# A hybrid GLA and attention step on one core: bounds of output rows and weights as sums of magnitudes on ScalarE, decays by their own exponential, another table of priorities

## The chip, the cores and the metric

The kernel runs on one core of one Trainium2 chip. The metric is the device time of one execution in microseconds (us); smaller is better. The engines of a core are named as the profile names them: PE (TensorE, matrix products; PEld are its weight loads), DVE (VectorE), ACT (ScalarE), POOL (GpSimd) and SP (SyncE, which only issues transfers here). Data is staged in SBUF; products land in PSUM banks of 128 x 512 fp32.

## The reference

One inference step through two layers, each adding its gated output to the rows `x` (256 context rows and 1024 sample rows of width 1024): bidirectional gated linear attention (GLA), then softmax attention. The part that the change touches is the GLA layer:

```python
def gla_mixer(h, w_in, wa1, wa2, ba, onorm, w_out, s0):
    proj = h @ w_in
    q, k, v, gate = jnp.split(proj, [...], axis=-1)
    def decay(d):
        z = ((h @ wa1[d]) @ wa2[d] + ba[d]).astype(jnp.float32)
        return (jax.nn.log_sigmoid(z) / GLA_TAU).reshape(B, T, GLA_HEADS, GLA_DK)
    o_f, s_f = gla_chunked(q, k, v, decay(0), s0[:, 0])
    o_b, s_b = gla_chunked(flip(q), flip(k), flip(v), flip(decay(1)), s0[:, 1])
    o = rms_norm(o_f + flip(o_b), onorm).reshape(B, T, GLA_VD).astype(h.dtype)
    y = (o * jax.nn.silu(gate)) @ w_out
```

Inside `gla_chunked` each chunk needs `exp(b)` and `exp(-b)` of the running sum `b` of the log decays, and the state is carried on by `exp(b_last)`.

## The kernel before

**Products.** Every large product is made from pairs of f16 numbers, `hi` and `lo`, whose sum is the fp32 value times a power of two; `mm3` (L242 to L247) issues three f16 matmuls for each piece of the inner dimension: hi by hi, lo by hi, hi by lo. To choose the power of two, a bound of the magnitudes is taken, and `pow2` (L198 to L222) turns it into a scale `s` and its inverse with a few one-column DVE instructions; for a weight block the bound is first carried across the partitions by a small matmul, called the cross below (L205). ACT then writes `hi` as a copy times `s`, and DVE writes `lo` as the rest. `fill_out` (L278) does this for the four 1 MB blocks of the output weights, wo0 to wo3, `out_prep` (L1046) for each 128 x 1024 piece of gated output rows; both take the bound as a maximum on DVE.

**GLA.** The layer runs over 4 heads x 10 pieces of 128 rows and a tail of 10 more slots, 50 slots in all (`gla`, L911). A slot makes, for pieces somewhat ahead, the decays (`decay`, L729: gates through `Abs`, `Exp`, `Ln` on ACT), their exponentials (`decayed`, L752: `en`, `ep` and the four end columns `eb`), and the value and gate products (`value_gate`, L707, whose gate half is read out of PSUM by ACT as `gx`, L718); for its own piece the inner products (`intra`, `kt` and `A`), the state update (`outer`), and, for the head before, the other direction (`combine`, with the state tile `Sc` on POOL) and the gated row (`gated`, L881, stored by SP as `og_d<-gx`). `filler` hangs other work on slots: conditioning products `gemv` (L425, matmuls that write 32 columns), weight blocks of the next layers, the output weights at slots 30, 32, 36 and 38, and the first six pieces of out_prep at slots from 40 on. `rank` (L647) is the low-rank product of the decays, also with 32 columns a matmul. Behind the slots comes `gla_out`, the output projection with the rest of out_prep, and then the attention layer.

**Order.** Nothing in the code fixes the order of an engine's instructions. The building program lists them by priority: the place in the code plus the offset that `LATER` gives to the part's name (`later`, L188), and each engine then runs its list in order. SP's list is at the same time the order of its transfer queue.

Of the kernel before, what the change touches and what calls it, by code (L numbers as in the profile page):

```python
# [9 lines left out]
F32 = mybir.dt.float32  # L10
I32 = mybir.dt.int32
AF = mybir.ActivationFunctionType
ALU = mybir.AluOpType
AX = mybir.AxisListType
# [3 lines left out]
P = 128  # L18
# [32 lines left out]
LATER = {  # L51
    "loc": -30,
    "kt": 30,
    "A": -375,
    "intra": -5,
    "ks": 10,
    "combine": -15,
    "cs": -40,
    "vg": -10,
    "u": 35,  # L60
    "gated": -20,
    "decay": -25,
    "outer": 5,
    "Uc": -140,
    "a9.qr": 100,
    "a.s1": 30,
    "gate": -5,
    "a0.key": -70,
    "x.qr": -120,
    "z.val": 205,  # L70
    "o": -130,
    "x.q": -15,
    "a0.qr": 145,
    "x.prep": 20,
    "oa": 60,
    "jobs": -20,
    "a.q": -215,
    "x.mod": -200,
    "x.res": -225,
    "a.val": -20,  # L80
    "a9.gate": -20,
    "a9.q": -185,
    "a.s0": -25,
    "a.qr": -205,
    "a9.s1": -60,
    "a0.s1": 340,
    "pieces8": 55,
    "filler": -25,
    "a0.s0": 75,
    "at": -110,  # L90
    "a0.rest": -5,
    "a0.gate": 130,
    "silu": -395,
    "a9.s0": -55,
    "x.setup": -180,
    "a9.val": 0,
    "combine9": 280,
    "jobs9": 220,
    "filler9": -10,
    "x.key8": -55,  # L100
    "eres": 45,
    "emod": -70,
    "wo2": 185,
    "fold": 55,
    "a0.q": 35,
    "wo3": 180,
    "x.key": -95,
    "s.v": 580,
    "s.q1": 185,
    "s.r0": -155,  # L110
    "s.n2": -490,
    "s.r1": 300,
    "gated9": 30,
    "eprep": 400,
    "x.kset": 170,
    "s.q0": -25,
    "s.s0": 45,
    "s.m1": -170,
    "s.s1": 245,
    "s.rk": -135,  # L120
    "s.n1": 0,
    "a9.val.3": -265,
    "a.s0.1": -55,
    "a9.val.1": -105,
    "a9.rest.0": 25,
    "a9.rest.2": -110,
    "a.rest.0": -35,
    "a.val.1": 25,
    "z.val.0": 55,
    "a.q.0": -110,  # L130
    "a9.qr.1": 45,
    "z.val.1": -25,
    "a9.gate.2": 255,
    "a9.s1.0": -175,
    "a9.q.0": -225,
    "a9.gate.0": 20,
    "a9.q.2": -120,
    "a9.s1.2": -105,
    "a.s0.3": -85,
    "a.s1.0": -30,  # L140
    "a9.gate.3": 20,
    "a9.s1.3": 185,
    "z.prep": 50,
    "a9.s0.0": -25,
}

ADA = tuple((0, b) for b in (8, 9, 10, 11)) + tuple((1, b) for b in (4, 5, 6, 7, 0, 1, 2, 3, 8, 9, 10, 11))
# [13 lines left out]
class K:  # L161
# [115 lines left out]

    def fill_out(self, w, st):  # L278
        nc = self.nc
        mx = self.t(self.small, [P, 2, 2], F32, "wmx")  # L280
        par = st.rearrange("p (q b j) n -> p q b j n", q=2, j=2)
        for q in range(2):
            for b in range(2):
                nc.vector.tensor_reduce(
                    mx[:, q, b : b + 1], par[:, q, :, b, :], AX.XY, ALU.max, apply_absolute_value=True
                )
        o2 = self.onorm.unsqueeze(1).to_broadcast([P, 2, 2])
        nc.vector.tensor_tensor(mx, mx, o2, ALU.mult)
        m = self.t(self.small, [P, 1], F32, "wm1")
        nc.vector.tensor_reduce(m, mx, AX.XY, ALU.max, apply_absolute_value=True)  # L290
        s, w[2] = self.pow2(m)
        so = self.t(self.small, [P, 2], F32, "wso", bufs=2)
        nc.vector.tensor_scalar(so, self.onorm, s, None, ALU.mult)
        for q in range(2):
            for b in range(2):
                hi, lo = (t.rearrange("p (q b j) n -> p q b j n", q=2, j=2)[:, q, :, b, :] for t in w[0:2])
                nc.scalar.activation(hi, par[:, q, :, b, :], AF.Copy, scale=so[:, b : b + 1])
                nc.vector.scalar_tensor_tensor(lo, par[:, q, :, b, :], so[:, b : b + 1], hi, ALU.mult, ALU.subtract)
# [453 lines left out]
    def decayed(self, h, i, g):  # L752
        nc = self.nc
        cs = self.bank("cs")[:, 0:260].rearrange("p (d k) -> p d k", d=2)
        with self.later("cs"):
            for d in range(2):
                for j in range(2):
                    nc.tensor.matmul(cs[:, d, :], g[j][:, d, :], self.cum[:, d, :], start=j == 0, stop=j == 1)
        en = self.t(self.ew, [P, 2, P], F32, "en")
        nc.scalar.activation(en, cs[:, :, 0:P], AF.Exp, scale=-1.0)  # L760
        ep = self.t(self.ew, [P, 2, 130], F32, "ep")
        nc.scalar.activation(ep, cs, AF.Exp)
        q, k = self.qkcol(h, 0, i), self.qkcol(h, 1, i)
        self.mark = nc.vector.tensor_tensor(en, en, k.unsqueeze(1).to_broadcast([P, 2, P]), ALU.mult).ins
        qe = self.t(self.tl, [P, 2, P], F32, "qe", bufs=NT + 1)
        nc.vector.tensor_tensor(qe, ep[:, :, 0:P], q.unsqueeze(1).to_broadcast([P, 2, P]), ALU.mult)
        eb = self.t(self.tl, [P, 2, 2], F32, "eb", bufs=NT + 2)
        nc.gpsimd.tensor_copy(eb, ep[:, :, P : P + 2])
        return {"qe": qe, "ke": en, "eb": eb}

    def intra(self, i, st):
# [274 lines left out]
    def out_prep(self, i, og, parts):  # L1046
        nc = self.nc
        mx = self.t(self.small, [P, 1], F32, "wm1")
        nc.vector.tensor_reduce(mx, og, AX.X, ALU.max, apply_absolute_value=True)
        s, inv = self.pow2(mx, cross=False)  # L1050
        hi, lo = parts
        nc.scalar.activation(hi, og, AF.Copy, scale=s)
        self.last = nc.vector.scalar_tensor_tensor(lo, og, s, hi, ALU.mult, ALU.subtract).ins
        to = [t[:, :, i * P : i * P + P] for t in (self.hT_hi, self.hT_lo)]
        nc.sync.dma_start_transpose(to[0], hi)
        self.tr = nc.sync.dma_start_transpose(to[1], lo).ins
        return *to, inv
# [897 lines left out]
```

## Time and profile before

| | before |
|---|---|
| time, median of 3 runs | 1244.21 us (1242.92 to 1245.89) |
| time of the profiled execution | 1240.44 us |
| its span | 1238.7 us |
| ACT busy | 684.6 us, 55% |
| POOL busy | 323.7 us, 26% |
| transfers | 210.14 MB, mean 170 GB/s |

The profile lists for each engine its busy time, for each group of instructions (line, engine, operation, names out<-in, partitions x elements) the count, the busy time, the mean of one in ns and the idle time of the engine just before them with what ended it. A row of the timeline gives the start in us, the duration, the engine, line and operation, and in brackets the idle time before it and what released it. The table by stretches gives for each stretch its length, each engine's busy time with its count, the granted PE clock as a share of the full one, the busy share of the transfer engines and their GB/s.

### The profile page before, as it was taken

The page shows a single profiled execution, that of the slowest core. Times are in us where ns is not written, and L with a number is a line of the kernel's source. Part 1 is how long each engine was busy: PE and PEld are TensorE (multiplying, and loading weights), DVE is VectorE, ACT ScalarE, POOL GpSimd, SP SyncE. Part 2 cuts the span into 40 slices and gives each one's busy share as a digit, 9 for nine tenths or more (in the row PEclk, how much of TensorE's full clock was granted, in tenths as well). Part 3 has the DMA queues.
Part 4 walks back from the last instruction along what each step waited for, and adds up shares of the span by engine and source line. Part 5 has one row for each costly group of instructions (what it writes and reads, how often), then busy time and mean ns, then how long its engine had stood idle before and what let it go on. Part 6 is the DMA issues. An engine that isn't in the chain of part 4 may idle for free. (4 is left out here: it accounts for less than half of the span.)

```text
span 1238.7 us, 22382 instructions
## 1 busy us (share of the span) xinstructions
PE 1190.6 (96%) x7990; PEld 779.1 (63%) x7990; DVE 941.7 (76%) x2177; ACT 684.6 (55%) x1694; POOL 323.7 (26%) x566
## 2 busy tenths in 40 slices
PE   5899999999999999799999999999999999989998
PEld 3467765655556566567776666766766667766444
DVE  4787778888788789986876877877767687796653
ACT  3574565666666657742333576666677676663100
POOL 0132122333221243310223444331332342310000
PEclk9999999999999999999999999999999999999999
DMA  9511567366555544479987896667957666889442
GB/s 381 215 48 74 196 195 237 113 198 203 175 186 171 184 136 144 124 189 308 205 192 187 186 174 137 134 132 145 191 126 156 128 118 137 193 152 240 153 136 85
DMA packets 318496, 210.14 MB, mean 170 GB/s; under 512 B 257158, under 2 KB 294702, under 8 KB 310064
## 3 DMA queue, kind: packets, MB, share of 16 engines
q1 hardware_dynamic: 311232, 191.18, 60.2%
q10 hardware_dynamic: 4688, 10.57, 2.3%
q0 software_dynamic: 2464, 6.95, 2.0%
q8 instruction: 63, 1.03, 0.4%
q14 instruction: 49, 0.40, 0.1%
HBM read 108.35 MB, written 38.96 MB: 119 GB/s over the span
## 5 line engine op out<-in xcount | busy, mean ns | idle before, releaser
L247 PEld LDWEIGHTS <-hT_hi 128*128 128x128 f16 x1920 | 187.6, 98 | 119.9 <-issue 3.8
L247 PE MATMUL mm<-whi,hT_hi 128*128 128x512 f16 (+1 forms) x576 | 200.1, 348 | 3.1 <-ACT gx L718 2.7
L247 PE MATMUL mm<-whi,hT_lo 128*128 128x512 f16 (+1 forms) x576 | 200.2, 347 | 0.0
L247 PE MATMUL mm<-wlo,hT_hi 128*128 128x512 f16 (+1 forms) x560 | 194.2, 347 | 0.7 <-DVE wlo L309 0.7
L247 PEld LDWEIGHTS <-whi 128*128 128x128 f16 x1232 | 120.2, 98 | 60.3 <-issue 0.9
L1344 PE MATMUL S<-kT,wst 128*128 128x512 f16 (+1 forms) x624 | 142.1, 338 | 6.5 <-ACT p L1352 6.5
L247 PE MATMUL mm<-hT_hi,whi 128*128 128x256 f16 (+1 forms) x480 | 141.0, 294 | 0.6 <-DVE og L1407 0.6
L247 PE MATMUL mm<-hT_lo,whi 128*128 128x256 f16 (+1 forms) x480 | 141.0, 294 | 0.0
L247 PE MATMUL mm<-hT_hi,wlo 128*128 128x256 f16 (+1 forms) x480 | 141.0, 294 | 0.0
L1382 DVE SCALAR_TENSOR_TENSOR phl<-p,srec,phl 128x1280 f16<-128x1280 f32 (+1 forms) x79 | 105.5, 1335 | 45.7 <-ACT phl L1381 28.4
L247 PEld LDWEIGHTS <-hT_lo 128*128 128x128 f16 x960 | 94.2, 98 | 61.3 <-issue 0.9
L1347 DVE TENSOR_REDUCE smx<-S 128x1 f32<-128x1280 f32 (+1 forms) x80 | 101.5, 1272 | 27.3 <-PE S L1344 27.1
L247 PE MATMUL mm<-PT,vh 128*128 128x256 f16 x672 | 114.8, 273 | 5.8 <-DMA PT<-phl 5.6
L1352 ACT ACTIVATE p<-S,snb,acol 128x1280 f32<-128x1280 f32 (+1 forms) x80 | 99.0, 1238 | 8.9 <-DVE phl L1382 3.8
L1344 PEld LDWEIGHTS <-wst 128*128 128x128 f16 x624 | 61.0, 98 | 57.0 <-issue 7.7
L247 PE MATMUL mm<-PT,vl 128*128 128x256 f16 x336 | 91.6, 273 | 0.0
L1379 POOL TENSOR_SCALAR phl<-p,srec 128x1280 f16<-128x1280 f32 (+1 forms) x40 | 53.7, 1342 | 104.6 <-DVE srec L1370 57.8
L247 PEld LDWEIGHTS <-wlo 128*128 128x128 f16 x616 | 60.2, 98 | 29.4
L247 PEld LDWEIGHTS <-vh 128*128 128x128 f16 x672 | 65.2, 98 | 16.0 <-DMA PT<-phl 4.4
L1172 POOL TENSOR_TENSOR rope<-hx,ropet 128x64 f32<-128x64 f32 x160 | 53.9, 367 | 76.2 <-ACT hx L1308 61.9
L270 DVE TENSOR_REDUCE wmx<-wst 128x1 f32<-128x512 f32 x104 | 65.2, 677 | 7.4 <-DMA wst<-in_att_w 5.2
L238 POOL TENSOR_TENSOR hrs<-hrsa,mhalf 128x2 f32<-128x2 f32 x50 | 40.1, 803 | 102.8 <-DVE hrsa L236 84.9
(383 smaller groups left out, 2681.0 us busy)
## 6 DMA issues: line engine op xcount, KB each, us to landing
wada<-in_w_ada SPq DMA_DIRECT2D x16, 1024.0 KB, 5.4
wst<-in_att_w SPq DMA_DIRECT2D x14, 1024.0 KB, 5.5
wst<-in_gla_w_in SPq DMA_DIRECT2D x12, 1024.0 KB, 5.5
og_d<-og POOLq DMA_DIRECT2D x40, 128.0 KB, 2.8
wst<-og_d SPq DMA_DIRECT2D x5, 1024.0 KB, 6.5
og_d<-gx SPq DMA_DIRECT2D x37, 128.0 KB, 2.1
xr<-x_d SPq DMA_DIRECT2D x9, 512.0 KB, 3.4
out<-xr ACTq DMA_DIRECT2D x17, 256.0 KB, 2.0
```

Source lines behind the costliest of these rows:

```text
L238: nc.gpsimd.tensor_tensor(r, a, self.mhalf[:, 0:w], ALU.pow)
L247: self.pe = self.nc.tensor.matmul(out, a, b, start=k == 0 and j == 0, stop=k == n - 1 and j == 2).ins
L270: nc.vector.tensor_reduce(mx[:, j : j + 1], st[:, 2 * j : 2 * j + 2, :], AX.XY, ALU.max, apply_absolute_value=True)
L1172: nc.gpsimd.tensor_tensor(tv[:, h, :, w, :], xv[:, h, :, 1 - w, :], sn[:, :, w, :], ALU.mult)
L1344: nc.tensor.matmul(S[:, a : a + n], x, y, start=m == 0, stop=m == 2)
L1347: last = nc.vector.tensor_reduce(mx, S, AX.X, ALU.max).ins
L1352: nc.scalar.activation(p, S, AF.Exp, scale=self.sexp, bias=nb, accum_out=den)
L1379: nc.gpsimd.tensor_scalar(hi, p, r, 2.0 ** 14, ALU.mult, ALU.mult)
L1382: nc.vector.scalar_tensor_tensor(lo, p, r2, hi, ALU.mult, ALU.subtract)
```

## The change

Three functions and the table. In `fill_out` the four DVE reduces of a block become two ACT instructions `Abs`, each over 128 x 1024 elements, that sum the magnitudes as they go; what they write goes into the block's `hi` tile and is overwritten there by the copies. The sum over both halves takes the place of the maximum. In `decayed` the second exponential covers the 256 columns only, and the four end columns get an exponential of their own instead of a POOL copy. In `out_prep` the DVE reduce becomes one ACT `Abs` with a sum, written into `hi`. Sums are never below the maxima, so `hi` and `lo` still fit, with another power of two.

```diff
@@ -277,17 +277,14 @@
 
     def fill_out(self, w, st):
         nc = self.nc
-        mx = self.t(self.small, [P, 2, 2], F32, "wmx")
+        mx = self.t(self.small, [P, 2], F32, "wmx")
         par = st.rearrange("p (q b j) n -> p q b j n", q=2, j=2)
-        for q in range(2):
-            for b in range(2):
-                nc.vector.tensor_reduce(
-                    mx[:, q, b : b + 1], par[:, q, :, b, :], AX.XY, ALU.max, apply_absolute_value=True
-                )
-        o2 = self.onorm.unsqueeze(1).to_broadcast([P, 2, 2])
-        nc.vector.tensor_tensor(mx, mx, o2, ALU.mult)
+        for b in range(2):
+            junk = w[0][:, 4 * b : 4 * b + 4, :].rearrange("p (q j) n -> p q j n", q=2)
+            nc.scalar.activation(junk, par[:, :, b], AF.Abs, accum_out=mx[:, b : b + 1])
+        nc.vector.tensor_tensor(mx, mx, self.onorm, ALU.mult)
         m = self.t(self.small, [P, 1], F32, "wm1")
-        nc.vector.tensor_reduce(m, mx, AX.XY, ALU.max, apply_absolute_value=True)
+        nc.vector.tensor_reduce(m, mx, AX.X, ALU.add, apply_absolute_value=True)
         s, w[2] = self.pow2(m)
         so = self.t(self.small, [P, 2], F32, "wso", bufs=2)
         nc.vector.tensor_scalar(so, self.onorm, s, None, ALU.mult)
@@ -758,14 +755,14 @@
                     nc.tensor.matmul(cs[:, d, :], g[j][:, d, :], self.cum[:, d, :], start=j == 0, stop=j == 1)
         en = self.t(self.ew, [P, 2, P], F32, "en")
         nc.scalar.activation(en, cs[:, :, 0:P], AF.Exp, scale=-1.0)
-        ep = self.t(self.ew, [P, 2, 130], F32, "ep")
-        nc.scalar.activation(ep, cs, AF.Exp)
+        ep = self.t(self.ew, [P, 2, P], F32, "ep")
+        nc.scalar.activation(ep, cs[:, :, 0:P], AF.Exp)
         q, k = self.qkcol(h, 0, i), self.qkcol(h, 1, i)
         self.mark = nc.vector.tensor_tensor(en, en, k.unsqueeze(1).to_broadcast([P, 2, P]), ALU.mult).ins
         qe = self.t(self.tl, [P, 2, P], F32, "qe", bufs=NT + 1)
-        nc.vector.tensor_tensor(qe, ep[:, :, 0:P], q.unsqueeze(1).to_broadcast([P, 2, P]), ALU.mult)
+        nc.vector.tensor_tensor(qe, ep, q.unsqueeze(1).to_broadcast([P, 2, P]), ALU.mult)
         eb = self.t(self.tl, [P, 2, 2], F32, "eb", bufs=NT + 2)
-        nc.gpsimd.tensor_copy(eb, ep[:, :, P : P + 2])
+        nc.scalar.activation(eb, cs[:, :, P : P + 2], AF.Exp)
         return {"qe": qe, "ke": en, "eb": eb}
 
     def intra(self, i, st):
@@ -1046,9 +1043,9 @@
     def out_prep(self, i, og, parts):
         nc = self.nc
         mx = self.t(self.small, [P, 1], F32, "wm1")
-        nc.vector.tensor_reduce(mx, og, AX.X, ALU.max, apply_absolute_value=True)
+        hi, lo = parts
+        nc.scalar.activation(hi, og, AF.Abs, accum_out=mx)
         s, inv = self.pow2(mx, cross=False)
-        hi, lo = parts
         nc.scalar.activation(hi, og, AF.Copy, scale=s)
         self.last = nc.vector.scalar_tensor_tensor(lo, og, s, hi, ALU.mult, ALU.subtract).ins
         to = [t[:, :, i * P : i * P + P] for t in (self.hT_hi, self.hT_lo)]
```

`LATER` gets other numbers for most names of the GLA stage and of the setup and for some of the last attention step (a9); two of some seventy lines:

```diff
-    "gated": -20,
+    "gated": 145,
...
-    "silu": -395,
+    "silu": -520,
```

The lines behind the first hunk move up by three, so L718 of before is L715 of the changed kernel. In the order of PE the setup, the output projection and the attention stay, but for one place in the last attention step; the GLA stage is in another order on every engine. Three places of it follow.

The first is SP's queue at the end of the GLA stage: `split` takes a row piece already stored to DRAM (`og_d`), `wlo<-gb_d` are two loads of 512 KB, and gx_6327 of before is gx_6323 of the changed kernel, the gated row of the same slot. Before:

```order
L882 DMA og_d_64<-gx_6203 128x256
L472 DMA gb_d_69<-gb_1621_6235 128x2x8 x2
L1795 DMA split_6583<-og_d_64 128x768
L501 DMA wlo_1746_6659<-gb_d_69 128x1024 x2
L882 DMA og_d_64<-gx_6327 128x256
L882 DMA og_d_64<-gx_6448 128x256
```

Changed:

```order
L1792 DMA split_6575<-og_d_64 128x768
L1784 DMA whi_1745_6650<-in_x_sample 128x1024
L469 DMA gb_d_69<-gb_1621_6231 128x2x8 x2
L1784 DMA whi_1745_6650<-in_x_sample 128x1024
L879 DMA og_d_64<-gx_6323 128x256
L498 DMA wlo_1746_6651<-gb_d_69 128x1024 x2
L879 DMA og_d_64<-gx_6442 128x256
L1792 DMA wst_6574<-og_d_64 128x768 x2
```

The store of that gated row stood behind the two row loads and stands ahead of them now; the next one (gx_6448, now gx_6442) stays behind them.

The second is ACT's list some slots later. gx is the read of a gate product, ls and junk are steps of its silu and a sum of squares, and q_ with wm_ is the new sum of magnitudes, L1047. Before, from the read gx_6757:

```order
L718 ACTIVATE gx_6757<-mm_6732,inv_g_1704_6501 128x256
L872 ACTIVATE junk_6774,ossq_6775<-og_6772 128x256
L351 ACTIVATE ls_6759<-gx_6757 128x256
L352 ACTIVATE ls_6759<-ls_6759 128x256
L353 ACTIVATE ls_6759<-ls_6759 128x256
L718 ACTIVATE gx_6823<-mm_6798,inv_g_1704_6501 128x256
L872 ACTIVATE junk_6840,ossq_6841<-og_6838 128x256
L351 ACTIVATE ls_6825<-gx_6823 128x256
L361 ACTIVATE ls_6759<-ls_6759 128x256
L352 ACTIVATE ls_6825<-ls_6825 128x256
L353 ACTIVATE ls_6825<-ls_6825 128x256
```

Changed, the same stretch; gx_6749, which answers to gx_6757, and a first sum (q_1747 with wm_1760) stand right ahead of it:

```order
L1047 ACTIVATE q_1765_6722,wm_1778_6774<-wst_6574 128x1024
L715 ACTIVATE gx_6815<-mm_6790,inv_g_1704_6495 128x256
L348 ACTIVATE ls_6751<-gx_6749 128x256
L869 ACTIVATE junk_6766,ossq_6767<-og_6764 128x256
L348 ACTIVATE ls_6817<-gx_6815 128x256
L349 ACTIVATE ls_6751<-ls_6751 128x256
L869 ACTIVATE junk_6832,ossq_6833<-og_6830 128x256
L1049 ACTIVATE q_1747_6656<-wst_6574,p2s_6714 128x1024
L1049 ACTIVATE q_1765_6722<-wst_6574,p2s_6780 128x1024
L349 ACTIVATE ls_6817<-ls_6817 128x256
L350 ACTIVATE ls_6751<-ls_6751 128x256
L715 ACTIVATE gx_6969<-mm_6944,inv_g_1704_6495 128x256
```

Between the reads gx_6749 and gx_6969 stand two sums and two copies of 128 x 1024 that were further down before.

The third is PE in the second rank product early in the GLA stage, mm_1324 (L647, now L644); mm_1297 is a full-width product. Before, from its first matmul:

```order
L647 LDWEIGHTS wa1h_472
L647 MATMUL mm_1324<-hT_hi_73,wa1h_472 32x256
L647 LDWEIGHTS wa1l_473
L647 MATMUL mm_1324<-hT_hi_73,wa1l_473 32x256
L247 LDWEIGHTS hT_lo_74
L247 MATMUL mm_1297<-whi_70_308,hT_lo_74 128x256
L647 LDWEIGHTS wa1h_472
L647 MATMUL mm_1324<-hT_lo_74,wa1h_472 32x256
L247 LDWEIGHTS hT_hi_73
L247 MATMUL mm_1297<-whi_70_308,hT_hi_73 128x256
L647 LDWEIGHTS wa1h_472
L647 MATMUL mm_1324<-hT_hi_73,wa1h_472 32x256
```

Changed, from its eighth matmul:

```order
L644 LDWEIGHTS wa1l_473
L644 MATMUL mm_1324<-hT_hi_73,wa1l_473 32x256
L644 LDWEIGHTS wa1h_472
L644 MATMUL mm_1324<-hT_lo_74,wa1h_472 32x256
L247 LDWEIGHTS hT_hi_73
L247 MATMUL mm_1297<-whi_70_308,hT_hi_73 128x256
L644 LDWEIGHTS wa1h_472
L644 MATMUL mm_1324<-hT_hi_73,wa1h_472 32x256
L247 LDWEIGHTS hT_hi_73
L247 MATMUL mm_1297<-wlo_71_309,hT_hi_73 128x256
L644 LDWEIGHTS wa1l_473
L644 MATMUL mm_1324<-hT_hi_73,wa1l_473 32x256
```

Before, two of its 24 matmuls came first, seven stood one by one between full-width matmuls, and 15 closed; now nine come first and the other 15 stand one by one. Of the 16 conditioning products `gemv`, two were cut in two by another product before (mm_3301, mm_3929), and five are now (mm_1498, mm_2665, mm_4472, mm_5146, mm_5433).

More of the change, by code (lines that the diff above doesn't have):

```diff
@@ L53 @@
     "kt": 30,
[L54 to L58, printed above, removed]
-    "vg": -10,
-    "u": 35,
-    "gated": -20,
-    "decay": -25,
-    "outer": 5,
-    "Uc": -140,
+    "A": -390,
+    "intra": -25,
+    "ks": 135,
+    "combine": -5,
+    "cs": -15,
+    "vg": -10,
+    "u": 30,
+    "gated": 145,
+    "decay": -35,
+    "outer": 20,
+    "Uc": -130,
     "a9.qr": 100,
@@ L70 @@
     "z.val": 205,
-    "o": -130,
+    "o": -30,
     "x.q": -15,
@@ L74 @@
     "x.prep": 20,
-    "oa": 60,
+    "oa": 30,
     "jobs": -20,
@@ L80 @@
     "a.val": -20,
-    "a9.gate": -20,
-    "a9.q": -185,
+    "a9.gate": 15,
+    "a9.q": -200,
     "a.s0": -25,
     "a.qr": -205,
-    "a9.s1": -60,
+    "a9.s1": -120,
     "a0.s1": 340,
     "pieces8": 55,
-    "filler": -25,
+    "filler": -40,
     "a0.s0": 75,
-    "at": -110,
+    "at": -75,
     "a0.rest": -5,
     "a0.gate": 130,
-    "silu": -395,
-    "a9.s0": -55,
+    "silu": -520,
+    "a9.s0": 60,
     "x.setup": -180,
     "a9.val": 0,
-    "combine9": 280,
-    "jobs9": 220,
-    "filler9": -10,
+    "combine9": 215,
+    "jobs9": 255,
+    "filler9": -50,
     "x.key8": -55,
-    "eres": 45,
-    "emod": -70,
+    "eres": 150,
+    "emod": -25,
     "wo2": 185,
-    "fold": 55,
+    "fold": 125,
     "a0.q": 35,
-    "wo3": 180,
+    "wo3": 205,
     "x.key": -95,
[L108 to L114, printed above, removed]
+    "s.v": 725,
+    "s.q1": 130,
+    "s.r0": -190,
+    "s.n2": -500,
+    "s.r1": 585,
+    "gated9": 50,
+    "eprep": 375,
     "x.kset": 170,
[L116 to L119, printed above, removed]
+    "s.q0": 15,
+    "s.s0": 115,
+    "s.m1": -165,
+    "s.s1": 305,
     "s.rk": -135,
-    "s.n1": 0,
-    "a9.val.3": -265,
+    "s.n1": 50,
+    "a9.val.3": -305,
     "a.s0.1": -55,
-    "a9.val.1": -105,
-    "a9.rest.0": 25,
-    "a9.rest.2": -110,
+    "a9.val.1": -65,
+    "a9.rest.0": 305,
+    "a9.rest.2": -145,
     "a.rest.0": -35,
@@ L132 @@
     "z.val.1": -25,
[L133 to L136, printed above, removed]
+    "a9.gate.2": 195,
+    "a9.s1.0": -180,
+    "a9.q.0": -365,
+    "a9.gate.0": -80,
     "a9.q.2": -120,
-    "a9.s1.2": -105,
+    "a9.s1.2": -295,
     "a.s0.3": -85,
     "a.s1.0": -30,
-    "a9.gate.3": 20,
-    "a9.s1.3": 185,
+    "a9.gate.3": 170,
+    "a9.s1.3": 230,
     "z.prep": 50,
-    "a9.s0.0": -25,
+    "a9.s0.0": 90,
 }
```

## The prediction

> **What bounds the kernel now.** I read first the page (engine totals), then the table by stretches of the span, then TensorE's (PE) own rows with the idle time ahead of them.
>
> ```profile
> span 1238.7 us, 22382 instructions
> PE 1190.6 (96%) x7990; PEld 779.1 (63%) x7990; DVE 941.7 (76%) x2177; ACT 684.6 (55%) x1694; POOL 323.7 (26%) x566
> ```
>
> ```profile
> core 0: us, PE busy (x) PEld busy (x) DVE busy (x) ACT busy (x) POOL busy (x), PEclk, DMA share, GB/s
> 83.00:487.00 404.00, 403.04 (x2514) 249.98 (x2512) 333.35 (x909) 247.63 (x651) 114.58 (x211) 1.00 0.52 168
> 487.00:523.00 36.00, 29.18 (x212) 22.70 (x212) 33.62 (x110) 25.75 (x68) 12.55 (x19) 0.95 0.45 138
> 523.00:700.00 177.00, 176.92 (x1302) 127.62 (x1303) 133.24 (x294) 67.88 (x176) 43.65 (x86) 1.00 0.87 211
> ```
>
> PE is busy for 403.0 of the 404 us of the GLA stage and for 176.9 of the 177 us of the gla_out stage behind it. There, work taken from VectorE (DVE), GpSimd (POOL) or ScalarE (ACT) is worth nothing by itself, and only what PE itself does, or waits for, counts. Between the two, from 487 to 523, PE has 29.2 busy us of 36. This seam is the only place touched by the change where PE visibly waits:
>
> ```profile
> 487.15 0.23 PE L758 MATMUL cs<-cum,ghi 128*128 128x130 f16 x1 [0.22 <-POOL ghi L747]
> ...
> 495.29 0.60 PE L865 MATMUL cs<-Sc,qe 128*128 128x256 f32 x2
> 496.59 0.23 PE L205 MATMUL z<-ident,wm 128*128 128x128 bf16 x1 [0.71 <-DVE wm L290]
> 499.48 0.37 PE L247 MATMUL mm<-whi,hT_hi 128*128 128x256 f16 x1 [2.66 <-ACT gx L718]
> ...
> 508.15 0.70 PE L865 MATMUL o<-Sc,qe 128*128 128x256 f32 x2 [0.53 <-POOL Sc L830]
> 509.49 0.70 PE L865 MATMUL U<-Sc,qe 128*128 128x256 f32 x2 [0.64 <-POOL Sc L830]
> 511.15 0.70 PE L865 MATMUL z<-Sc,qe 128*128 128x256 f32 x2 [0.97 <-POOL Sc L830]
> 522.05 0.39 PE L247 MATMUL A<-whi,hT_hi 128*128 128x512 f16 x1 [1.04 <-DMA hT_hi<-q]
> ```
>
> The brackets sum to 6.77 us. They begin at a modelled end; from start to start a gap is longer: the pair at 495.29 has two passes of 0.216, so the next start was due at 495.72 and came at 496.59, 0.87 late where the bracket has 0.71. With 0.16 for each of seven gaps the seam loses 7.9 us. Behind the longest gap the clock is halved as well:
>
> ```profile
> 495.70:499.40 3.70, 0.41 (x2) 0.95 0.55 209
> 499.40:502.50 3.10, 3.02 (x15) 0.51 0.00 0
> 1091.00:1094.00 3.00, 0.51 (x4) 1.00 0.86 213
> ```
>
> From 499.4 to 502.5 PE had a granted clock of 0.51 and got through 15 matmuls in 3.1 us, 0.21 each; at the full clock a 128x256 half of this kind starts every 0.11. That is 1.5 us more: the seam costs **9.4 us** in all.
>
> Why the 2.66 wait: the read of the gate columns (gx, L718) that frees the PSUM bank stood on ACT until a store had landed and its buffer was free.
>
> ```profile
> 498.96 0.47 ACT L718 ACTIVATE gx<-mm,inv_g 128x256 f32<-128x256 f32 x1 [2.90 <-DMA og_d<-gx]
> ```
>
> ```profile
> 491.10 0.42 SPq L1795 DMA_DIRECT2D split<-og_d  x1
> 491.69 0.86 SPq L501 DMA_DIRECT2D wlo<-gb_d  x2
> 492.79 4.03 SPq L882 DMA_DIRECT2D og_d<-gx  x2
> ```
>
> The store og_d<-gx was issued at 492.79, behind 384 KB of split<-og_d and two row loads wlo<-gb_d of 512 KB each on the same queue, and ACT was released only at 498.96, 6.2 us later.
>
> **The change, part by part.** (1) DVE and POOL lose work, ACT gets it:
>
> ```profile
> L284 DVE TENSOR_REDUCE wmx<-wst 128x1 f32<-128x512 f32 x16 | 10.2, 678 | 0.4 <-DMA wst<-in_gla_w_out 0.4
> L1049 DVE TENSOR_REDUCE wm<-wst 128x1 f32<-128x1024 f32 x5 | 6.1, 1213 | 2.2 <-DMA wst<-og_d 2.2
> ```
>
> ```profile
> L508 ACT ACTIVATE hl<-xr 128x1024 f16<-128x1024 f32 x8 | 8.4, 1054 | 16.1 <-DVE xr L1030 14.7 <-DMA xr<-in_x_prompt 1.4
> L1349 ACT ACTIVATE snb<-smx,acol 128x1 f32<-128x1 f32 x80 | 23.0, 288 | 45.9 <-DVE smx L1347 45.8
> L760 ACT ACTIVATE en<-cs 128x256 f32<-128x256 f32 x40 | 15.3, 383 | 0.9 <-PE cs L758 0.9
> L297 ACT ACTIVATE whi<-wst,wso 128x512 f16<-128x512 f32 x12 | 7.7, 709 | 1.4 <-DVE wso L293 1.4
> L351 ACT ACTIVATE ls<-gx 128x256 f32<-128x256 f32 x80 | 33.3, 416 | 3.7 <-DVE g L743 1.8 <-DVE gx L362 0.8
> ```
>
> DVE loses the 16 reduces of fill_out (16 x 0.678 = 10.8 us) and the 10 of out_prep (10 x 1.213 = 12.1). ACT gets 8 + 10 magnitude sums of 128x1024; no such row is in the trace, the nearest is L508's 1.054, also an f16 write of 1024 with a sum, so 18 x 1.05 = 19 us. It also gets 40 exponentials of four columns, between L1349's 0.288 for one column and L760's 0.383 for 256: 12 to 15 us, and I take 12. In the GLA stage ACT goes from 248 to about 268 of 404 us, two thirds: PE hides it, at 0. Without that cover the 40 exponentials alone would cost 12; nothing below 0 is possible where PE has no gap. In gla_out the six other out_prep sums (6.3 us) lie on an ACT that is busy for 68 of 177: 0 again. The bounds become sums, so scales are other powers of two; no instruction depends on it.
>
> (2) The table LATER moves PE's rows in the GLA stage. What costs there is only what PE itself runs differently. Two kinds of matmul write 32 columns and are quick only among themselves:
>
> ```profile
> 107.77 0.28 PE L647 MATMUL mm<-hT_hi,wa1l 128*32 128x256 f16 x1
> 107.98 0.28 PE L247 MATMUL mm<-whi,hT_lo 128*128 128x256 f16 x1
> 108.20 0.28 PE L647 MATMUL mm<-hT_lo,wa1h 128*32 128x256 f16 x1
> ...
> 111.20 0.28 PE L647 MATMUL mm<-hT_hi,wa1h 128*32 128x256 f16 x1
> ...
> 111.65 0.27 PE L647 MATMUL mm<-hT_lo,wa1h 128*32 128x256 f16 x1
> ```
>
> ```profile
> 249.14 0.62 PE L425 MATMUL mm<-wada,cst 128*32 128x256 f32 x2
> 249.69 0.28 PE L733 MATMUL z<-wa,r 98*128 98x256 f16 x1
> 249.91 1.06 PE L425 MATMUL mm<-wada,cst 128*32 128x256 f32 x14
> 250.90 0.23 PE L758 MATMUL cs<-cum,ghi 128*128 128x130 f16 x1
> ...
> 286.78 1.07 PE L425 MATMUL mm<-wada,cst 128*32 128x256 f32 x16
> 287.79 0.23 PE L758 MATMUL cs<-cum,ghi 128*128 128x130 f16 x1
> ```
>
> In the second rank product (L647, 24 matmuls) each one that alternates with a full-width matmul has starts 0.215 apart, 0.43 for a pair, while the closing run of 15 starts all of its rows within 0.45 us (111.20 to 111.65). One that stands alone costs 0.43, less 0.11 for the full-width one and 0.03 for a place in a run (0.45 over 14): 0.29 more. Before, a run of 2 leads, 7 stand alone and 15 close; now 9 lead and 15 stand alone: 8 x 0.29 = 2.3, less some 0.3 for the entry and exit of the run that goes: **+2.0**. The ada product (L425, 16 passes) takes 1.01 in one piece (286.78 to 287.79) and 0.55 + 0.99 when something stands in it, the intruder itself starting 0.22 rather than 0.11 apart: +0.64. Two of the sixteen are cut now, five after: **+1.9**. Bounds: 0 if the intruder's place hides it, 6 if every cut costs twice.
>
> One wait in the stage goes:
>
> ```profile
> 221.15 0.41 PE L781 MATMUL kt<-ident,en 128*128 128x128 f32 x2 [0.83 <-DVE p2e L216]
> ```
>
> Behind that ada product kt waited 0.83; an A product stands there now, whose inputs are older: **-1.0** with the refill.
>
> (3) The seam. On SP's queue the store that ACT waited for now stands ahead of the two row loads, so the 2.66, the 0.71 (wo3's bound is now made on ACT some 10 us before its cross) and the half clock should go; the Sc updates now run in pairs of buffers, which takes 0.53, 0.64 and 0.97. But ACT, 25.8 of 36 us busy, gets four of the sums. Walking its new queue from one bank read to the next: between gx_6749 and gx_6969 lie two sums (2.1, with their reads 0.2 more), two 128x1024 copies (like the sums, 2.1), five steps of ls and two squares (7 x 0.416 = 2.9), gx_6815 and gx_6969 (0.9): 8.2 us, about 7.6 to 8.2 with overlapping starts. PE has 48 half matmuls (5.2) and three state pairs (1.3) between the two banks: 6.5. It waits 1.1 to 2.5 at mm_7066; I take 1.8. Between gx_6683 and gx_6749 lie four copies of wo3 (L297, 2.8), six ls, two squares (3.3) and a gx (0.5): 6.6 against 3.5 of PE with some 2 us in hand, 0.6 to 2.5 at mm_6944; I take 1.5. Two smaller ones (en_6406 behind wo3's sum, gx_6615 behind wo2's copies) 0.7. After: **4.0**, with 1 and 9 as ends (1: ACT's queue is never late; 9: as much as now). -9.4 + 4.0 = **-5.4**.
>
> (4) The last attention step: one score pair moves behind a gate product, on PE alone. Waits there end on DVE or on transfers: 0, +-0.5.
>
> **Sum**: -5.4 + 2.0 + 1.9 - 1.0 = -2.5 us. The profiled execution of before took 1240.4 (span plus 1.7), 3.8 below the median; I carry the difference over: 1244.2 - 2.5 = **1241.7**.
>
> A rule that weighs the 1.5 us of half clock: the Trainium skill, "TensorE: Matmul & The Clock Gate", Part 1, says the clock is granted by a free-running window of about 3.4 us, so a gap hits it by phase. The trace agrees that 3.7 us of near idleness lost it and that 3.0 us at 1091 did not. By that rule the other runs of before may not pay the 1.5, and the sum would be -1.0 instead of -2.5.
>
> **Rivals.** *A: ACT keeps up at the seam* and only 1 us remains: -8.4 + 3.9 - 1.0 = -5.5, **1238.7**. For it: ACT idles 10 of those 36 us. Against: its new rows come in one clump between two bank reads.
> *B: ACT takes the place of the queue* (the slower one). gx_6683 must wait for the store of gx_6442, which is now the one behind the two row loads, and the sums come on top: 9 us of waits, and one of them, over the 3.0 us that the trace bore and near the 3.7 that it did not, halves the clock again (1.5). 10.5 - 9.4 + 3.9 - 1.0 = +4.0, **1248.2**. It decides once gx_6749 comes over 3 us late. For it: 6.2 us from issue to landing. Against: PE has those 2 us in hand ahead of gx_6683.
> *C: nothing comes of it*: the seam keeps 6.5 us since one store still lands behind the loads and PE is full elsewhere: -2.9 + 3.9 - 1.0 = 0, **1244.2**.
> A rule that speaks for C: the Trainium skill, "DMA: Bandwidth & Descriptors", on HWDGE ordering, says descriptors of one issuing engine are taken in ring order on each DMA engine. The trace agrees (a store held 6.2 us behind 1.4 MB); by it whichever store is second pays.
>
> **How the numbers follow.** A measurement of this kernel tells about 0.2% (2.5 us) from no change: faster is below 1241.7, slower above 1246.7. Forecast 0.42 (1239.5 to 1244, half of it faster, half the same); A 0.22 (faster); C 0.18 (same, 0.03 of it slower); B 0.18 (slower, 0.02 of it the same). So faster 0.43, same 0.38, slower 0.19. The range leaves out the outer half of A and of B: 1237.5 to 1248.
>
> **What would show it.** In the profile of the changed kernel: PE's brackets between 487 and 523 sum to 3 to 4 instead of 6.8, with ACT gx as the releaser and no Sc; the clock there stays at 1.00; no bracket at the kt behind the ada product; single 128*32 rows alternate 15 times in the rank product, and five ada groups are cut. DVE falls by 23 us, POOL's eb copies are gone, ACT rises by about 31. Wrong would be PE waits inside 100 to 480, which this working holds to be none, or a granted clock of 0.5 at the seam.

## The result, and the profile after

The changed kernel takes 1247.0 us (median of 22 runs, 1241.99 to 1252.84), the kernel before 1242.84 on the same chip (22 runs, 1239.41 to 1248.91): 1.0030 times, with a 95% interval of 1.0016 to 1.0043. It is slower by about 4 us, where 2.5 us less was forecast. The profiled execution of the changed kernel took 1248.2 us (span 1246.4), 7.7 us of span more than the one of before; part of that is chance of one execution, as the experiments show.

First the engines' totals on the page of the changed kernel, then its table by the stretches that were used for before (length, then busy time and count for each engine, granted clock, share and GB/s of the transfers):

```profile
span 1246.4 us, 22389 instructions
PE 1196.6 (96%) x7990; PEld 779.6 (63%) x7990; DVE 924.1 (74%) x2151; ACT 705.6 (57%) x1770; POOL 315.0 (25%) x526
```

```profile
83.00:487.00 404.00, 401.62 (x2467) 245.27 (x2466) 328.54 (x896) 256.35 (x698) 103.86 (x170) 1.00 0.52 166
487.00:523.00 36.00, 35.67 (x272) 29.21 (x272) 31.68 (x113) 32.25 (x84) 15.18 (x21) 1.00 0.62 172
523.00:700.00 177.00, 172.16 (x1262) 123.89 (x1261) 118.37 (x270) 69.55 (x172) 41.02 (x78) 0.99 0.84 206
```

The middle row is the seam: PE is now busy for 35.7 of 36 us, at the full clock, although ACT is busy for 32.3 of them. The row below is where the time went: in the output projection PE was busy for 176.9 of 177 us and is now for 172.2. The first row has lost a little as well. PE's waits in the table of waits (engine, line, what it waited for, us in total, times, longest), first for 430 to 535 us, then for 560 to 660; in the second stretch the kernel of before has no row at all:

```profile
PE o L862 <- POOL Sc L825: 2.2, 1, 2.2
PE A L247 <- DMA hT_lo<-k: 0.3, 1, 0.3
```

```profile
PE kv L247 <- DMA wkv<-w_kv: 2.7, 2, 2.3
PE y L247 <- DMA hT_lo<-oghl: 2.2, 2, 1.9
```

Two milestones divide the gain from the loss: the first key/value product (kv) in the middle of the output projection, and the first score product (S) at its end. In two profiles of before kv starts at 579.4 and 579.9, in two of the changed kernel at 577.1 and 577.6: up to there the change **gains 2.3 us**. S starts at 695.5 and 696.0 before and at 700.4 and 701.0 after: between the two the change **loses 7.2 us**. From S to the last product it is 539.1 and 542.7 before, 542.0 and 541.4 after; these sums can't be told apart, though one wait inside them did grow, as the account below shows. The first two together, 4.9 us later at S, are near the 4.2 between the medians.

### The profile page after: what moved, and what is told of

It reads as the page before. It is cut to its first block, busy times and chain, and to the rows that moved or that the text cites. A ratio compares the mean times of both kernels' runs of the same rounds, so it can differ in the third digit from the quotient of the medians.

```text
span 1246.4 us, 22389 instructions
## 1 busy us (share of the span) xinstructions
PE 1196.6 (96%) x7990; PEld 779.6 (63%) x7990; DVE 924.1 (74%) x2151; ACT 705.6 (57%) x1770; POOL 315.0 (25%) x526
```

## The experiments

Each kernel is compared with runs of before on the same chip; ratios are to those. The start of S is read from one profile of each. A half clock below is a stretch in which the granted clock falls to about 0.5.

**1. The table of before on the changed functions, and 2. the changed table on the functions of before.** Which of the two parts costs?

```diff
-    "gated": 145,
+    "gated": -20,
...
-    "emod": -25,
+    "emod": -70,
```

This is the first, two of its lines; all numbers of LATER are those of before. The second is the reverse, on the kernel of before.

> The changed kernel's three functions with the table LATER of before. Theory T1 (three sources: the new table cuts packed groups of 32-column matmuls, +3.9 us, and puts o ahead of a late Sc, a 2.2 us wait with half a clock behind it; the sums of out_prep on ScalarE wait there for loads and hold up what is behind them, 5.5 us of PE waits after 575): the rank product keeps its closing run of 15 and only two ada products are cut, so the start of the first score product (695.5 before, 700.4 changed) falls by 4 to 8 us as far as the table goes, while waits for wkv and hT_lo between 575 and 650 stay, some 3 to 5 us. Rival T2 (the loss lies in the attention stage, where nothing was moved, and differs from run to run): the start of the first score product stays within 2 us of 700.4 and the time at 1247. Rival T3 (ScalarE's 20 more busy us cost wherever they lie): no gain from the table, 1247.

> The kernel of before with the new table LATER alone. T1: seven ada products are cut instead of two and the rank product ends in 15 single matmuls, together +5 us of PE work in the GLA stage, and no waits of PE for wkv or for hT_lo of oghl in the output projection over 1 us, since the bounds of out_prep are still VectorE's: start of the first score product 695 to 699, depending on the seam. T2: the start at 695.5 +-1. T3: as before, 1243.

Measured: 1260.22 us (1.0119, 1.0098 to 1.0141) with S at 713.4, and 1255.18 us (1.0089, 1.0072 to 1.0107) with S at 707.6. None of the three theories had this: each half alone is 11 to 15 us slower, both together 4. The packing did follow the table as T1 said (run of 15 kept and two ada groups cut in the first; single matmuls and seven cuts in the second), but waits outweigh it. In the first, PE's table of waits for 430 to 690 us begins:

```profile
PE kv L247 <- DMA whi<-w_kv: 10.2, 1, 10.2
PE o L862 <- POOL Sc L825: 2.7, 1, 2.7
```

In the second, PE still waits 3.2 us for gx near the seam. So neither the table nor the functions gain anything alone. That the offsets fit the durations of the functions for which they were found is a reading of this; no run tests it by itself.

**3. out_prep's bound on VectorE again**, all ten pieces:

```diff
-        nc.scalar.activation(hi, og, AF.Abs, accum_out=mx)
+        nc.vector.tensor_reduce(mx, og, AX.X, ALU.max, apply_absolute_value=True)
```

> The changed kernel with the bound of out_prep as VectorE's maximum again; the order of the GLA stage stays as it is up to its end. T1: the waits for wkv (2.7 us) and hT_lo of oghl (2.2 us), and the half clock behind them, are gone; start of the first score product 700.4 - 7 = 693 to 695, time 1247 - 6 = 1240 to 1242. T2: time within 1.5 us of the changed kernel. T3: as T2, since ten sums are 12 us of 706 on ScalarE.

> The changed kernel once more, for what comes again in a second profile. T1: the wait of o for Sc near 440 (2.2 us), of kv for wkv near 582 (2.7) and of y for hT_lo near 628 (2) come again, start of the first score product 700.4 +-1.5. T2: the waits before the attention are chance and go or move by more than 2 us each. Both: 1247 +-1.5.

Number 4 is the changed kernel, unedited. Measured: 1246.72 (1.0017, 1.0001 to 1.0033) for number 3 and 1246.83 (1.0023, 1.0009 to 1.0037) for number 4. Number 4's profile repeats all three waits, 2.6 us at 441.6, 2.9 near 582 and 1.8 for hT_lo, so they are no chance. In number 3, S started at 697.2, earlier by 3.5 but not by 7: the wait for wkv was gone, but one of 2.2 us for hT_lo stayed, although no sum of out_prep is on ACT there, and 1.8 us came up at the seam, whose order had shifted. The medians show nothing of it. Undoing the part as a whole changes too many places, SP's queue among them.

**5, 6 and 7: two causes, apart and together.** Number 5 puts VectorE's maximum back for the four pieces inside the output projection only; PE, POOL and SP keep their order. (`late_prep` is set where the output projection begins.)

```diff
-        nc.scalar.activation(hi, og, AF.Abs, accum_out=mx)
+        if len(og.shape) == 2 and self.late_prep:
+            nc.vector.tensor_reduce(mx, og, AX.X, ALU.max, apply_absolute_value=True)
+        else:
+            nc.scalar.activation(hi, og, AF.Abs, accum_out=mx)
```

Number 6 leaves the functions as they are and moves one priority of the table, that of the early rows' norm. It changes SP's queue and leaves PE's and POOL's order; in ACT's and DVE's lists a few instructions between 530 and 600 us change places as well:

```diff
-    "emod": -25,
+    "emod": -120,
```

Number 7 does both.

> The changed kernel with VectorE's maximum for the four pieces that out_prep bounds inside the output projection, and ScalarE's sums for the six early ones; PE's, GpSimd's and SyncE's orders stay as they are. Theory T1 (the four sums stand at the head of ScalarE's list until a load of og, or the transposes of two pieces before, are done, 24 us in all, and hold up the next piece's norm): PE's waits of 5.5 us for wkv and hT_lo between 575 and 650 fall by 3 us or more, start of the first score product 700.7 - 3.5 = 697, time 1244. Rival T4 (SyncE's order: 3.5 MB of loads now stand ahead of the transposes of the second early row piece): the waits stay within 1 us of 5.5, start 700 to 701, time 1247.

> The changed kernel with the priority of the early rows' norm (emod) at -120: PE's order stays, on SyncE the two transposes of split and a load of xr and og come ahead of the loads of w_kv and of the rotary table, as before the change; ScalarE's sums stay. T4: PE's waits between 575 and 650 go (under 1 us), no half clock there, start of the first score product 694 to 695, time 1241. T1: the waits stay at 5 to 6 us, or move from wkv to a later piece; start 700 +-1.

> Both edits, VectorE's maxima for the four late pieces and emod at -120. T1 and T4 together: no wait over 0.5 us between 575 and 650, start of the first score product 700.7 - 7.3 = 693.4, time 1247 - 6 = 1241, faster than before. If only one of the two causes is real, this gives the same as that edit alone.

PE's waits between 560 and 660 us in number 5, in number 6 and in number 7, in that order:

```profile
PE kv L247 <- DMA wkv<-w_kv: 2.8, 2, 2.3
```

```profile
PE y L247 <- DMA hT_lo<-oghl: 3.5, 2, 2.3
PE kv L247 <- DMA wlo<-w_kv: 0.2, 1, 0.2
```

```profile
PE kv L247 <- DMA wlo<-w_kv: 1.1, 1, 1.1
PE kv L247 <- DMA whi<-w_kv: 1.0, 1, 1.0
```

With the changed kernel these are four cases. The wait for wkv is gone once SP's order is moved (6 and 7), the waits for hT_lo are gone once the late sums are off ACT (5 and 7). But the sums are not the only source of a wait for hT_lo: numbers 3 and 9 have one of 2.2 and 2.0 us without any late sum on ACT.

Times: 1243.54 (1.0002, 0.9988 to 1.0016), 1246.39 (1.0028, 1.0015 to 1.0042) and, for both, **1240.73 us** (0.9983, 0.9968 to 0.9997); S at 696.0, 695.2 and 694.6. Number 7 is the fastest of these kernels, by 0.2% against the one of before and with an interval that only just leaves out no change.

The starts of S hold more than the work of the edits. Up to 530 us all engines of numbers 5, 6 and 7 run the lists of the changed kernel, and yet near 440 us o waited only 1.4, 0.9 and 1.8 us for Sc there, without a half clock, instead of 2.2 and 2.6 us with one. So these three profiles were 2 to 4 us ahead before their edits could act, by chance (in number 6 half of it from the first 50 us). A stretch without this is that from M to S, where M is the first matmul (of a y product) from which PE's list up to S is the same in all these kernels:

| kernel | M | S | M to S |
|---|---|---|---|
| before, two profiles | 549.48, 549.94 | 695.54, 696.00 | 146.1, 146.1 |
| changed, two profiles | 547.18, 547.61 | 700.42, 701.02 | 153.2, 153.4 |
| 5, late sums off ACT | 545.19 | 696.02 | 150.8 |
| 6, emod moved | 543.05 | 695.18 | 152.1 |
| 7, both | 544.43 | 694.60 | 150.2 |

Of the 7.2 us lost there, number 5 gives back 2.4, number 6 1.1 and number 7 3.1. In number 5 the time and the start of S came out as T1 had them, but the waits between 575 and 650 fell by 2.1 us, not 3, and 2 us of the earlier S were chance. In number 6 both theories were half right: wkv went, hT_lo stayed and even grew, and against the expectation of T4 the time did not improve measurably. In number 7, 2.1 us of waits remained where none over 0.5 was expected, with a half clock behind them: whi<-w_kv is issued at 568.12 for a kv product that PE reaches near 574.5, in the kernel of before at 560.25 for one at 579.43.

How ACT's sums delay hT_lo is in its table of waits for 560 to 640 us and its rows, both of the changed kernel:

```profile
ACT oghl L1047 <- DMA og<-og_d: 17.4, 2, 10.4
ACT hl L516 <- DVE xr L514: 12.4, 4, 4.6
ACT oghl L1047 <- DMA hT_lo<-oghl: 6.6, 2, 4.4
```

```profile
580.31 1.06 ACT L1047 ACTIVATE oghl<-og 128x1024 f16<-128x1024 f32 x1 [10.37 <-DMA og<-og_d]
...
581.36 1.04 ACT L505 ACTIVATE hl<-xr 128x1024 f16<-128x1024 f32 x1
```

The sum over a piece stands 10.4 us at the head of ACT's list until its load has landed, and the norm of another row piece (hl<-xr, L505) starts in the next microsecond after it. In the profile of before the same norm ran at 572.30, nine us sooner. Not all of that is the sum's: in number 5, with the sum off ACT and SP's order unchanged, the norm starts at 575.91, after a wait for SP's transposes of split:

```profile
575.91 1.06 ACT L505 ACTIVATE hl<-xr 128x1024 f16<-128x1024 f32 x1 [8.23 <-DMA hT_hi<-split]
```

That is 5.5 us sooner than in the changed kernel, 2 of them the chance above. Further down, the transposes hT_lo<-oghl of the second piece are issued at 613.46 in number 5 and at 622.82 in the changed kernel, where PE waits for them at 627.8. VectorE's maximum stood in DVE's list at a place where the load had long landed, and its rows have no such wait.

**8. The kernel of before once more.**

> The kernel of before once more, for a second profile: start of the first score product 695.5 +-1; from there to the last product 539.0 in the first profile. If the 2.5 us that the changed kernel is longer there are its own, 539 +-0.7 comes again and no half clock behind the wait near 1094; if they are chance, 541 to 542.

1244.61 us; S at 696.0, then 542.7 us to the last product, somewhat more than the 541 to 542 that were to mean chance. So most of the 2.5 us was chance: this profile, too, has the clock down behind the wait at 1095 (0.67 in the stretch below, first two numbers its start and end), which the first did not, and once more behind one at 1143.6. The wait itself is longer in the changed kernel, as the account below shows.

```profile
1095.30:1099.00 3.70, 3.70 (x24) 0.67 0.87 165
```

**9 and 10: the packing**, on top of number 7, by the priority of filler, which carries the rank product and the ada products:

```diff
-    "filler": -40,
+    "filler": -120,
```

Number 10 has -50 there.

> e7_both with the priority of filler at -120 instead of -40: the second rank product is one run of 24 matmuls and one ada product is cut instead of five; the rest of the GLA stage is listed anew around that. If packing costs what the terms of the sum say: rank 5.2 - 1.0 = 4.2 us less than in the changed kernel and ada 4 x 0.64 = 2.6 less, start of the first score product 694.6 - 6.8 = 688, time 1240.7 - 6.8 = 1234, provided that no new wait comes. Rival: the time of a packed group is only moved to a wait elsewhere (PE waits for VectorE or ScalarE instead), and the start stays at 693 to 696, time 1240 to 1242.

> e7_both with filler at -50: a run of 19 and five single matmuls in the second rank product, one ada product cut. Packing: rank 10 x 0.29 = 2.9 less, ada 2.6 less, start of the first score product 689, time 1235.5. Rival: as in e9, 693 to 696 and 1240 to 1242.

Measured: 1242.15 (0.9991, 0.9970 to 1.0012) and 1245.4 us (1.0003, 0.9982 to 1.0024), S at 693.2 and 695.7. In number 9 the 24 rank matmuls are one run from 107.54 to 108.53, 1.0 us, as worked out, against 6.87 us with 15 full-width matmuls among them in the changed kernel. But of 6.8 us expected 1.4 arrived at S: the new list has waits of its own, 0.7 us at 141, 2.7 us at 165.9 and 2.0 us for hT_lo at 603, with a half clock behind each of the last two. Number 10 has waits of 1.8 us at 143 and of 2.3 at 439.8, each with a half clock behind it. The rival was nearer in both, though the time of number 10 is above its 1240 to 1242 as well.

**11. The state loaded into its own tile**, on top of number 7. The row that makes o wait at 440.8 in the changed kernel, with SP's queue and POOL:

```profile
440.81 0.70 PE L862 MATMUL o<-Sc,qe 128*128 128x256 f32 x2 [2.19 <-POOL Sc L825]
```

```profile
433.99 0.34 SPq L837 DMA_DIRECT2D out<-s  x1
438.09 3.04 SPq L824 DMA_DIRECT2D s<-in_state_gla  x2
```

```profile
440.29 0.48 POOL L825 TENSOR_SCALAR Sc<-s,eb 128x256 f32<-128x256 f32 x1 [7.34 <-DMA s<-in_state_gla]
```

The state load shares one buffer with the store of a final state: the store goes out at 433.99, the load follows at 438.09 (SP's table of waits has it stand 3.7 us for the store), Sc at 440.29, and o at once behind it.

```diff
-            s0 = self.t(self.ew, [P, DV], F32, "s0", bufs=1)
-            nc.sync.dma_start(s0, self.I["state_gla"][0, 0, d, h])
-            nc.gpsimd.tensor_scalar(s, s0, eb[:, d, 0:1], 1.0, ALU.mult, ALU.mult)
+            nc.sync.dma_start(s, self.I["state_gla"][0, 0, d, h])
+            nc.gpsimd.tensor_scalar(s, s, eb[:, d, 0:1], 1.0, ALU.mult, ALU.mult)
```

> e7_both with the carried-in state loaded into the state tile itself and scaled there, so that its load no longer waits until the store of a final state has freed the one buffer s0. If the 2 us wait of o for Sc near 440 comes from that buffer: no wait over 0.5 us and no half clock there, start of the first score product 694.6 - 3.5 = 691, time 1237. Rival: the load is late for its place on SyncE's queue, or for the state tile, and the wait stays within 0.7 us of 1.9.

The wait near 440 and the half clock are gone, as was expected if the buffer was the cause, though number 9 has no such wait either and keeps the buffer in another order; and the time is 1258.73 us (1.0120, 1.0097 to 1.0143). From 430 to 600 us PE has:

```profile
PE kv L247 <- DMA whi<-w_kv: 13.7, 1, 13.7
PE kv L247 <- DMA wlo<-w_kv: 1.2, 1, 1.2
```

The list of the stage had come out anew, and the loads of w_kv were issued at 574.8, in the changed kernel at 564.9. It is the same place that cost number 1 ten microseconds. Why the list put them there was not tried.

**12. A scratch tile for the sums**, on top of number 6:

```diff
-        nc.scalar.activation(hi, og, AF.Abs, accum_out=mx)
+        if self.late_prep:
+            junk = self.t(self.xp, [P, D], F16, "pjunk", bufs=1)
+        else:
+            junk = hi
+        nc.scalar.activation(junk, og, AF.Abs, accum_out=mx)
```

> e6_emod_first with ScalarE's sums in the output projection writing their values into a scratch tile of their own instead of the hi tile of the piece, which is one of two buffers; part of the output projection is listed anew. In e6_emod_first ScalarE stood 6.9 us on the transposes that still read that buffer and 16.4 us on the loads of og. If the buffer is what makes hT_lo late: the 6.9 go, PE's waits of 2.4 and 1.4 near 604 and 623 go to under 0.5 each, start of the first score product 695.2 - 3.5 = 691.7. Rival: the loads are: ScalarE stands 16 us or more on og<-og_d, PE's waits for hT_lo stay at 2 us or more, start 694 to 697.

1254.47 us (1.0087, 1.0061 to 1.0112), with most of the excess in an attention stage whose order this edit changed too. For the question asked, one row of ACT's waits (560 to 640) and one of PE's (540 to 690) decide for the rival:

```profile
ACT pjunk L1052 <- DMA og<-og_d: 23.0, 4, 12.0
```

```profile
PE y L247 <- DMA hT_lo<-oghl: 3.5, 2, 2.0
```

The wait for the buffer is gone and the wait for the loads has grown from 16.4 to 23.0; hT_lo comes as late as before. So the tile that is written is not what makes it late in this order.

## Why the prediction was wrong

The forecast was 2.5 us faster; the kernel is about 4 us slower. By the prediction's own steps:

- **Work taken from VectorE and GpSimd is worth nothing by itself**: not contradicted, and no run shows it alone. DVE is busy 17.6 us less (23 had been worked out), POOL 8.7 less, ACT 21 more (31 had been worked out; the 40 small exponentials took 0.185 us each, where 0.3 was taken).
- **The packing**: right in size. The second rank product costs 6.87 us with 15 full-width matmuls among it against 4.09 with eight before, less the seven at 0.11: +2.0 as forecast. A cut ada group still costs 0.55 + 0.99 instead of 1.00, five times instead of two: +1.9. These rows of the changed kernel show a cut:

```profile
204.02 0.62 PE L422 MATMUL mm<-wada,cst 128*32 128x256 f32 x2
204.58 0.28 PE L730 MATMUL z<-wa,r 98*128 98x256 f16 x1
204.79 1.06 PE L422 MATMUL mm<-wada,cst 128*32 128x256 f32 x14
205.78 0.70 PE L848 MATMUL A<-v,at 128*128 128x256 f32 x2
```

- **The wait at 221 goes, -1.0**: right; an A product follows that ada product at once.
- **The seam, -5.4**: the waits went, and more of them than forecast, but the reason given does not show. In the brackets from 487 to 523 0.3 us is left, and the clock stays at 1.00; from start to start that is 0.5 against 9.4, a gain of about 9. The store does stand ahead of the row loads now, but it still takes 4.8 us from issue to landing and lands at 498.4, where ACT was released at 498.96 before. The read of gx that had waited for it (the 32nd in both kernels) comes only at 502.63, without a wait, and PE has other products until then. Rows of SP and ACT in the changed kernel:

```profile
493.57 0.38 SPq L879 DMA_DIRECT2D og_d<-gx  x1
```

```profile
502.63 0.48 ACT L715 ACTIVATE gx<-mm,inv_g 128x256 f32<-128x256 f32 x1
```

  Nor does the store that is second now (issued at 496.15) cost anything: the read that needs it, at 503.91, has no wait either. So PE's and ACT's new order covers the landing; whether the store's new place is needed was not tried. The 4.0 us of waits from the walk along ACT's list did not come, and rival A was nearer here: ACT kept up.
- **"PE hides it, at 0"** for the GLA stage missed one wait, o for Sc at 440.8, 2.2 us and a half clock behind it (0.57 in the stretch below); a wait inside 100 to 480 was one of the prediction's own signs of being wrong. "o" moved from -130 to -30 in the table and now stands where it needs a state whose buffer is freed only by a store. I had walked the distances between PE's own steps, not the carried-in state's load. The rows beside number 11 show that chain. The cost differs from run to run, from a wait of 0.9 us without a half clock to 2.6 with one, on the same list.

```profile
442.40:445.90 3.50, 3.50 (x11) 0.57 0.94 281
```

- **"In gla_out the six other out_prep sums (6.3 us) lie on an ACT that is busy for 68 of 177: 0 again"** is the step that failed: from M to S the changed kernel loses 7.2 us, 4.9 of them PE's waits for wkv and hT_lo, and most of the rest a half clock behind the wait for wkv. (Of the ten pieces six are early, so four lie in the output projection.) A free engine is no cover: what counts is which instructions of its list stand ahead of a wait. The sum needs a load, ACT takes its list in order, and the norm behind it came some 3 us later for it; number 5 shows this part, 2.4 us from M to S. The other part is SP's queue, which I compared only at the seam, and whose order elsewhere the prediction put at nothing without a reason: the same table moved the transposes of the second early row piece behind 1.5 MB (hT_hi) and 3.5 MB (hT_lo) more of loads. Number 6 undoes that and the wait for wkv goes, for 1.1 us by itself, since the waits for hT_lo grew. The two together, number 7, give back 3.1 us. The other 4 us are waits for w_kv in number 7 as well, and a half clock: PE comes earlier to kv than before the change, and the loads are issued later. Whether the rest of SP's new order is the reason stays open. The half clock of the changed kernel:

```profile
584.20:588.00 3.80, 3.80 (x24) 0.66 0.97 245
```

- **The last attention step, 0**: too small by a little. The wait of PE for PT<-phl near 1100 us is longer in both profiles of the changed kernel, 3.45 and 3.56 us against 2.60 and 2.74 before. It is 3.2 to 4.0 in every other run with the new numbers of the table, 2.3 in number 1, which has the old ones. First before, then changed:

```profile
1094.11 0.39 PE L247 MATMUL mm<-PT,vh 128*128 128x256 f16 x2 [2.60 <-DMA PT<-phl]
```

```profile
1100.75 0.60 PE L247 MATMUL mm<-PT,vh 128*128 128x256 f16 x2 [3.45 <-DMA PT<-phl]
```

  That is some 0.8 us; the rest of what the profiles differ behind S is mostly half clocks, which come and go from run to run.

Rival B's time, 1248.2, was nearest, and for none of its reasons: its place, the seam, is where the change gained most.

The change as it stands is a sum of gains of some 9 us at the seam and 1 at 221 and of losses of 3.9 by packing, some 4 at the state (in the two profiles of the changed kernel) and 7 in the output projection. The two last are not its aim, and of the 7 number 7 has 3 back. Its median is 6 us below that of the changed kernel; its profile has 3.1 of that from M to S and 2.8 ahead of M, most of it the luck at the state.

## What to carry to other kernels

Moving a reduction of a loaded tile from one engine to another moves its wait for the load as well; on the new engine everything listed behind it waits too, however idle the engine is on average. A priority table and the functions that it orders belong together: either half alone was three to four times as bad here as both together, so a part of such a change can't be judged by undoing it, only by edits that leave the other lists as they are. A start time late in one profile holds the chance of everything ahead of it; compare from the first instruction behind which the lists are the same. And when a table moves, compare every queue from the first moved row to the last, not only at the places that waited before.

## What the runs showed of the hardware that was not expected

The granted clock fell behind shorter gaps than those that the prediction took as safe, and stayed up behind longer ones. By the brackets, it went to 0.57 behind a wait of 2.19 us at 440.8 in the changed kernel and to 0.50 behind one of 1.78 us at 143.3 in number 10. It kept 1.00 behind one of 2.60 us at 1094 in the first profile of before and behind one of 3.44 us at 1097 in number 9. The stretch behind the wait in number 10, then that in number 9:

```profile
143.80:147.20 3.40, 3.40 (x13) 0.50 0.64 260
```

```profile
1097.00:1101.00 4.00, 4.00 (x38) 1.00 0.61 115
```

So a wait of about 2 us may cost 1.7 us more (3.4 us at half speed) or nothing, from run to run. The Trainium skill ("TensorE: Matmul & The Clock Gate", Part 1) says that half rate comes after at least one idle window of about 3.4 us, and that the window runs freely. The traces agree that a gap is hit by chance: the same list kept the clock behind 2.60 us in the first profile of before and lost it behind 2.74 in the second. They do not agree that a whole window has to be idle: 1.78 us were enough in number 10.
